# Gates, q and k as seven half products a pair, ahead of an attention in two token halves

## The chip, the core and the metric

The kernel runs on one core of a Trainium2 chip. The metric is the device time of one execution in microseconds (us); it is 1275.96 us before the change (median of 3 runs, 1275.76 to 1276.05). The engines are TensorE (PE in the profile, with its weight loads as PEld), VectorE (DVE), ScalarE (ACT), GpSimd (POOL) and SyncE (SP). SP and POOL also issue the DMA transfers; sixteen DMA engines move the bytes of both.

## The reference

One layer on 1024 tokens of width 1024, all in float32. What matters of it:

```python
h = rmsnorm(x, g_pre_mix)
proj = einsum('bsd,de->bse', h, w_in)            # u | q | k | v, 512 columns each
y_pool = einsum('bsc,cd->bsd', multiscale_pool(u_pool, w_pool_mix, pool_scale), w_br_pool)
# stick-breaking attention, 8 heads of 64, s < t only:
#   A[t,s] = sigmoid(z_ts) * prod_{s<j<t} (1 - sigmoid(z_tj)),  z = q k / 8,  o = A v
y_sb = einsum('bsc,cd->bsd', o_sb, w_br_sb)
gates = sigmoid(einsum('bsd,de->bse', h, w_gate) + b_gate)        # 2048 columns
merged = gates[..., :1024] * y_pool + gates[..., 1024:] * y_sb
x = x + rmsnorm(einsum('bsd,de->bse', merged, w_out), g_post_mix)
a = square(relu(einsum('bsd,df->bsf', rmsnorm(x, g_pre_mlp), w_up)))   # 4096 columns
x = x + rmsnorm(einsum('bsf,fd->bsd', a, w_down), g_post_mlp)
```

## The kernel before

**Layout and precision.** Activations lie transposed, channels on the 128 partitions and tokens along the free dimension, in two halves of 512 tokens. Every float32 operand is split into a rounded high part and the rest (`hi`, `lo`, both of the matmul type float32r), and every product is three matmuls: high x high, high x low, low x high (`mm3`, lines 107 to 117). A dense product of one 128-column group for one token half is 8 steps of three (`dense_steps`). The splits are a cast on ScalarE and a subtraction on VectorE.

**Who orders the work.** The program is written with a framework that allots buffers, sets every wait, and orders each engine's instructions: a planner plays the program through on a modelled time, and an engine gets the earliest written instruction that is ready then. On the chip each engine then runs its list strictly in that order, and so do the DMA queues of SP and POOL. `issue_after(i)` puts an instruction behind `i` on its engine.

**Stages.** `phase_in` loads x, splits it, and forms the four u groups, then q and k of the first pair of heads, with the pool windows on VectorE beside them. `phase_attention` runs over the 8 heads; for each, all eight rows of 128 query tokens: `att_scores` (z by two matmuls, then `F` = sigmoid(-z) and `T` = sigmoid(z) on ScalarE, a mask on POOL, a running product of F by a scan on VectorE, line 574, and a multiply of T by the shifted F, line 578), then `att_steps`, which transposes T on PE, splits it (lines 599 and 600) and multiplies it with v. Between these, a list of filler jobs (`fill`, `fillers`, `pump`) puts the other dense products: v, the other q and k pairs (`job_qk`) and the 16 gate groups (`job_gate`, each for both token halves, stored to DRAM as `gscr`). `phase_post` forms the branch products, multiplies them with the gates loaded back, merges, and forms the output product; `phase_mlp` and `down` follow.

**Seven products instead of eight.** The up product (from its second part on) and the down product use a seven-product scheme for 2 x 2 blocks. For the down product the sums of weight blocks are made ahead by DMA alone: `weight_sums` yields 32 transfers of 1 MiB from DRAM to DRAM on the POOL queue (line 1069 copies, line 1067 adds into the destination), into `wscr`. Before the change they are issued one at a time: after every second row of the attention scores, and the last four in `phase_post`.

```python
for add, out, src in (
    (False, s3, (0, 0)), (False, s1, (1, 0)), (True, s3, (1, 0)), (True, s1, (1, 1)),
    (False, s2, s3), (True, s2, (1, 1)), (False, s4, s2), (True, s4, (0, 1)),
):
    for q in range(4):
        ...
```

**PSUM.** Eight banks: two for dense products (`dps`), and in `zps` three for z, two for transposes, one for the attention's output.

Of the kernel before, what the change touches and what calls it, by code (L numbers as in the profile page):

```python
# [52 lines left out]
class Block:  # L53
    def __init__(self, tc, x, w, wmix, vec, eye, eyeb, maskb, rcnt, out):
# [3 lines left out]
        self.sched = []  # L58
# [4 lines left out]
        self.cut = 1024  # L63
        self.marks = []


    def prep(self, key, g, pieces=(), load=None, stash=None):
        nc = self.nc
        raw = self.wp.tile([P, 1024], F32, name="wraw", tag="wraw", bufs=2)
        if stash is None:  # L70
            hi = self.wp.tile([P, 1024], F32R, name="whi", tag="whi", bufs=3)
            lo = self.wp.tile([P, 1024], F32R, name="wlo", tag="wlo", bufs=3)
        else:
            t = self.hp.tile([P, 2, 1024], F32R, name="stash", tag=stash)
            hi, lo = t[:, 0, :], t[:, 1, :]
        edges = [0] + list(pieces) + [1024]
        for a, b in zip(edges, edges[1:]):
            c = slice(a, b)
            nc.sync.dma_start(raw[:, c], self.w[g][:, c])
            if load is not None:  # L80
                load()
            n = min(b - a, self.cut)
            for i in range(a, b, n):
                c = slice(i, i + n)
                nc.scalar.copy(hi[:, c], raw[:, c])  # L85
                self.last_lo = nc.vector.tensor_sub(lo[:, c], raw[:, c], hi[:, c].bitcast(F32)).ins  # L86
        self.prepped[key] = (hi, lo)
# [19 lines left out]
    def mm3(self, ps, terms, first=True, last=True):  # L107
        nc = self.nc
        n = len(terms)
        for i, (wh, wl, rh, rl) in enumerate(terms):  # L110
# [6 lines left out]
            nc.tensor.matmul(ps, wl, rh, start=False, stop=last and i == n - 1)  # L117
# [54 lines left out]
    def build(self):  # L172
        tc, nc = self.tc, self.nc
        self.table_inst = None
        order = [(("u", g), O_U + g) for g in (0, 1, 2, 3)]
        order += [(("q", 0), O_QK), (("k", 0), O_QK + 1)]
        self.fill = {
            -1: [("g", 0)],
            0: [("g", 8), ("g", 1)],
            1: [("q", 1), ("k", 1), ("g", 9)],  # L180
            2: [("g", 2), ("g", 10), ("g", 3, 0)],
            3: [("q", 2), ("k", 2), ("g", 3, 1), ("v", 0, 4)],
            4: [("v", 4, 32), ("g", 11)],
            5: [("g", 4), ("q", 3), ("k", 3)],
            6: [("g", 12), ("g", 5), ("g", 13, 0)],
            7: [("g", 13, 1), ("g", 6), ("g", 14), ("g", 7, 0)],
            8: [("g", 7, 1), ("g", 15)],
        }
        order += [(("v", 0, j), O_V + j) for j in range(2)]
        for h in range(-1, 9):  # L190
            for f in self.fill[h]:
                if f[0] == "v":
                    if f[1] == 0:
                        order += [(("v", 1, j), O_V + 2 + j) for j in range(2)]
                elif f[0] == "g":
                    if f[-1] != 1 or len(f) == 2:
                        order.append((f[:2], O_G + f[1]))
                else:
                    order.append((f, O_QK + 2 * f[1] + (f[0] == "k")))
        order += [(("br", e), O_BR + e) for e in range(8)]  # L200
        kept = {3: "t2_hi", 4: "t2_lo"}
        order += [(("out", 0, e), O_OUT + e, (), None, kept.get(e)) for e in range(8)]
        order += [(("out", 1, e), O_OUT + e) for e in (2, 1, 0)]
# [13 lines left out]
        self.wsums = self.weight_sums()  # L217
# [31 lines left out]


    def phase_in(self):
        tc, nc = self.tc, self.nc
        pa = tc.alloc_tile_pool(name="in_a", bufs=1, side="right")
        xs = [pa.tile([P, NK, H], F32, name=f"x{h}") for h in range(2)]
        mean = pa.tile([P, P], F32, name="mean")
# [1136 lines left out]
```

## Time and profile before

| | |
|---|---|
| time, median of 3 runs | 1275.96 us |
| span of the profiled execution | 1274.1 us |
| granted TensorE clock, mean | 1.000 |
| DMA packets moved | 233.70 MB, 183 GB/s on the mean |
| of it on the POOL queue (q0) | 88.49 MB, 23.7% of sixteen engines' span |
| of it on the SP queue (q1) | 144.04 MB, 33.9% |
| VectorE busy, 100 to 460 us (attention) | 278.75 of 360 us |
| ScalarE busy, 100 to 460 us | 199.00 of 360 us |

The page gives the busy time of each engine, the chain of work that ended last, and groups of instructions by line. A matmul's busy time overlaps that of its neighbours, since they are pipelined; the distance from one start to the next is what it costs. [...]

### The profile page before, as it was taken

The page shows a single profiled execution, that of the slowest core. Times are in us where ns is not written, and L with a number is a line of the kernel's source. Part 1 is how long each engine was busy: PE and PEld are TensorE (multiplying, and loading weights), DVE is VectorE, ACT ScalarE, POOL GpSimd, SP SyncE. Part 2 cuts the span into 40 slices and gives each one's busy share as a digit, 9 for nine tenths or more (in the row PEclk, how much of TensorE's full clock was granted, in tenths as well). Part 3 has the DMA queues.
Part 4 walks back from the last instruction along what each step waited for, and adds up shares of the span by engine and source line. Part 5 has one row for each costly group of instructions (what it writes and reads, how often), then busy time and mean ns, then how long its engine had stood idle before and what let it go on. Part 6 is the DMA issues. An engine that isn't in the chain of part 4 may idle for free.

```text
span 1274.1 us, 16614 instructions
## 1 busy us (share of the span) xinstructions
PE 1266.1 (99%) x6043; PEld 1057.7 (83%) x6043; DVE 924.9 (73%) x1315; ACT 614.6 (48%) x1022; POOL 169.6 (13%) x314
## 2 busy tenths in 40 slices
PE   9999999999999999999999999999999999999998
PEld 6898888889888888888878888888888888888887
DVE  8787688786878747551777988877775655776975
ACT  8235455564555542232456646455454433344452
POOL 1002213221223121100101002212120000001000
PEclk9999999999999999999999999999999999999999
DMA  6254447694686138671529578656559546556551
GB/s 226 67 165 166 146 161 163 138 219 141 124 215 223 67 120 232 198 219 33 182 85 303 183 247 277 219 198 208 199 205 346 193 154 223 189 179 238 199 220 67
DMA packets 75729, 233.70 MB, mean 183 GB/s; under 512 B 8608, under 2 KB 11168, under 8 KB 73472
## 3 DMA queue, kind: packets, MB, share of 16 engines
q1 hardware_dynamic: 48352, 144.04, 33.9%
q0 software_dynamic: 27152, 88.49, 23.7%
q8 instruction: 47, 0.77, 0.2%
q14 instruction: 34, 0.28, 0.1%
q10 hardware_dynamic: 144, 0.13, 0.0%
HBM read 178.10 MB, written 83.89 MB: 206 GB/s over the span
## 4 chain that ended last, share of the span: by engine, by line
PE 94%; DVE 3%; issue 1%; ACT 1%; DMA 1%; POOL 0%; SPq 0%; DVEq 0%; ACTq 0%; POOLq 0%
PE d L116 20%; PE d L117 20%; PE d L115 20%; PE dg L117 4%; PE dg L116 4%; PE dg L113 4%; PE o L616 3%; PE at L591 2%; PE dqk L116 2%; PE dqk L117 2%; PE dqk L113 1%; PE z L564 1%; PE z L561 1%; DVE F L574 1%; PE dv L117 1%
## 5 line engine op out<-in xcount | busy, mean ns | idle before, releaser
L116 PE MATMUL d<-blo,whi 128*128 128x512 f32 (+1 forms) x456 | 172.3, 378 | 0.0
L117 PE MATMUL d<-bhi,wlo 128*128 128x512 f32 (+1 forms) x456 | 171.9, 378 | 0.0
L115 PE MATMUL d<-bhi,whi 128*128 128x512 f32 (+1 forms) x456 | 168.7, 378 | 0.0
L574 DVE TENSOR_TENSOR_SCAN F<-F,past 128x256 f32<-128x256 f32 (+2 forms) x96 | 94.2, 981 | 20.9 <-ACT F L565 20.0
L85 ACT CAST whi<-wraw 128x512 fp32r<-128x512 f32 (+1 forms) x88 | 67.7, 799 | 77.2 <-PE d L116 38.0
L113 PE MATMUL dg<-hT_hi,whi 128*128 128x512 f32 x253 | 101.7, 402 | 0.0
L117 PE MATMUL dg<-hT_hi,wlo 128*128 128x512 f32 x256 | 100.8, 394 | 0.0
L116 PE MATMUL dg<-hT_lo,whi 128*128 128x512 f32 x256 | 100.4, 392 | 0.0
L117 PEld LDWEIGHTS d<-bhi,wlo 128*128 128x128 f32 x456 | 85.8, 188 | 15.9
L116 PEld LDWEIGHTS d<-blo,whi 128*128 128x128 f32 x456 | 85.7, 188 | 15.9
L115 PEld LDWEIGHTS d<-bhi,whi 128*128 128x128 f32 x456 | 85.5, 188 | 16.1
L86 DVE TENSOR_TENSOR wlo<-wraw,whi 128x512 fp32r<-128x512 f32 (+1 forms) x88 | 77.7, 905 | 28.4 <-ACT whi L85 28.3
L116 PE MATMUL d<-b_lo,whi 128*128 128x512 f32 x196 | 76.2, 390 | 0.4 <-DVE b_lo L836 0.4
L115 PE MATMUL d<-b_hi,whi 128*128 128x512 f32 x196 | 75.6, 389 | 0.0
L565 ACT ACTIVATE F<-z 128x256 f32<-128x256 f32 (+2 forms) x96 | 47.2, 493 | 58.8 <-DVE T L578 34.4
L117 PE MATMUL d<-b_hi,wlo 128*128 128x512 f32 x196 | 74.7, 389 | 0.0
L1124 DVE TENSOR_TENSOR wlo<-slots_hi,whi 128x1024 fp32r<-128x1024 f32 x29 | 35.5, 1225 | 53.1 <-ACT whi L1122 53.1
L600 DVE TENSOR_TENSOR alo<-at,ahi 128x512 fp32r<-128x512 f32 (+1 forms) x96 | 52.0, 553 | 29.9 <-ACT ahi L599 28.8
L1122 ACT CAST whi<-slots_hi 128x1024 fp32r<-128x1024 f32 x29 | 30.5, 1052 | 84.5 <-PE d L116 71.5
L599 ACT CAST ahi<-at 128x512 fp32r<-128x512 f32 (+1 forms) x96 | 45.1, 482 | 47.4 <-PE at L591 44.0
L1122 ACT CAST whi<-slots_lo 128x1024 fp32r<-128x1024 f32 x27 | 28.4, 1053 | 73.4 <-PE d L116 59.7
L578 DVE TENSOR_TENSOR T<-T,F 128x255 f32<-128x255 f32 (+3 forms) x96 | 53.1, 556 | 11.0 <-POOL T L568 2.5
(323 smaller groups left out, 3309.3 us busy)
## 6 DMA issues: line engine op xcount, KB each, us to landing
wraw<-w SPq DMA_DIRECT2D x80, 512.0 KB, 4.3
wscr<-w POOLq DMA_DIRECT2D x24, 1024.0 KB, 10.0
ext_b<-ascr SPq DMA_DIRECT2D x40, 512.0 KB, 4.3
gscr<-gs POOLq DMA_DIRECT2D x32, 256.0 KB, 4.2
gate<-gscr POOLq DMA_DIRECT2D x16, 512.0 KB, 4.5
pscr<-p SPq DMA_DIRECT2D x32, 256.0 KB, 3.2
braw<-w SPq DMA_DIRECT2D x16, 512.0 KB, 5.1
ascr<-c POOLq DMA_DIRECT2D x32, 256.0 KB, 5.0
```

Source lines behind the costliest of these rows:

```text
L85: nc.scalar.copy(hi[:, c], raw[:, c])
L86: self.last_lo = nc.vector.tensor_sub(lo[:, c], raw[:, c], hi[:, c].bitcast(F32)).ins
L113: nc.tensor.matmul(ps, wh, rh, start=first and i == 0, stop=False)
L115: nc.tensor.matmul(ps, wh, rh, start=first and i == 0, stop=False)
L116: nc.tensor.matmul(ps, wh, rl, start=False, stop=False)
L117: nc.tensor.matmul(ps, wl, rh, start=False, stop=last and i == n - 1)
L565: nc.scalar.activation(f[:, c : c + n], z[:, :n], AF.Sigmoid, scale=-1.0)
L574: nc.vector.tensor_tensor_scan(fr, fr, past[:, c : c + n][:, ::-1], 1.0 if top else f[:, c + n : c + n + 1], ALU.mult, ALU.max)
L578: nc.vector.tensor_mul(tl[:, c:e], tl[:, c:e], f[:, c + 1 : e + 1])
L599: nc.scalar.copy(hi[:, c:], at[:, c:])
L600: nc.vector.tensor_sub(lo[:, c:], at[:, c:], hi[:, c:].bitcast(F32))
L1122: last_split[0] = nc.scalar.copy(hi, src).ins
```

## The change

The parts of the work between the u products and the output product are rearranged.

- After u, v is formed for both token halves with 512 columns at once, scaled, and stored to DRAM (`vscr`). u too goes to DRAM (`uscr`).
- A new stage `phase_project` forms gates, q and k before the attention, as 12 pairs of output groups by seven half products. The activations' sums are made on VectorE in `phase_in`; the weights' sums are made by DMA (`sw_sums`, 24 transfers of 1 MiB, DRAM to DRAM) and loaded a pair ahead (`sw_weights`). Results go to DRAM (`qscr`, `gscr`).
- Beside these products a generator `later` loads v twice, one token apart, stores the split difference (`sscr`), computes the pool mixer from `uscr` (to `yscr`), and splits the branch and output weights and stores both parts (`hscr`). What passes through on-chip memory in it uses four staging buffers in turn (`staged`).
- The 32 transfers of `weight_sums` are issued in this stage, four behind the first result of each of the first eight pairs.
- The attention runs over all heads for the first 512 tokens, then over all heads for the others, with q and k loaded per head (`load_head`). It keeps only the running products of sigmoid(-z) and multiplies them with the differences of v; the second sigmoid, the mask and the multiply are gone. Fillers are now the pool branch products (`job_pool`), and in the second half the merge (`job_merge`) and output products (`job_out`) of the first token half. Branch and output weights come from `hscr`, already split.
- `phase_post` keeps the second token half. In the MLP the buffers of one stage are placed elsewhere.

```diff
+    PAIRS = [("q", 0), ("k", 0), ("q", 1), ("k", 1)] + [("g", i) for i in range(8)]
+    def sw_sums(self):
+        for n in range(3):
             ...
+            for out, x, y in ((s3, a21, a22), (s1, a11, a21), (s2, s3, a11), (s4, s2, a12)):
+                yield nc.gpsimd.dma_start(out, x)
+                yield nc.gpsimd.dma_start(out, y, accum_op=ALU.add)
+    def staged(self, shape, dt, name):
+        self.turn += 1
+        return self.mx.tile(shape, dt, name=name, tag=f"m{self.turn % 4}")
+    def result(self, kind, f, h, t, sign):
         ...
+        if kind == "g":
+            nc.scalar.activation(t, t, AF.Sigmoid, bias=self.vt[:, V_BG + f : V_BG + f + 1], scale=sign)
+            return nc.gpsimd.dma_start(self.gscr[f][:, c], t)
         ...
+        e = self.staged([P, 2, H], F32R, f"{kind}s")
         ...
+        return nc.gpsimd.dma_start(self.qscr[kind == "k"][f][:, :, c], e.bitcast(F32))
+    def later(self):
+        for t in range(NK):
+            pair = self.staged([P, 2, H], F32, "vpair")
+            for j in range(2):
+                nc.sync.dma_start(pair[:, j, :], self.vscr[t * P + j : t * P + j + P, :])
+            yield
             ...
+            nc.gpsimd.dma_start(self.sscr[t], v.rearrange("p h x -> p (h x)").bitcast(F32))
+            yield
         ...
+        for g in range(16):
+            raw = self.staged([P, 1024], F32, "hraw")
+            nc.sync.dma_start(raw, self.w[O_BR + g])
+            yield
+            hi, lo = (self.staged([P, 1024], F32R, "hw") for _ in range(2))
+            nc.scalar.copy(hi, raw)
+            nc.vector.tensor_sub(lo, raw, hi.bitcast(F32))
+            for t, scr in zip((hi, lo), self.hscr[g]):
+                nc.gpsimd.dma_start(scr, t.bitcast(F32))
+            yield
+    def phase_project(self):
         ...
+        def product(w, at, name):
+            pool, tag, n = next(banks)
+            d = pool.tile([P, H], F32, name="sw", tag=tag, bufs=n)
+            self.half(d, w, at, name)
+            next(nxt, None)
+            if i > 0:
+                next(bg, None)
+            return d
+        for i, (kind, f1) in enumerate(self.PAIRS):
             ...
+            nc.scalar.copy(u, product(w["a1"], 0, "b11"))
+            nc.vector.tensor_add(c11, u, product(w["a1"], 512, "b21"))
+            done = self.result(kind, f1, 0, c11, 1.0)
+            for _ in range(4):
+                with tc.issue_after(done.ins):
+                    next(self.wsums, None)
+            nc.vector.tensor_add(u, u, product(w["sb"], 0, "t2"))
+            nc.vector.tensor_add(v, u, product(w["sa"], 0, "t3"))
+            d = product(w["sa"], 512, "t1")
+            nc.vector.tensor_add(c22, v, d)
+            nc.vector.tensor_add(u, u, d)
+            self.result(kind, f2, 1, c22, -1.0)
+            nc.vector.tensor_add(v, v, product(w["a22"], 0, "t4"))
+            self.result(kind, f2, 0, v, -1.0)
+            nc.vector.tensor_add(u, u, product(w["sb"], 512, "b22"))
+            self.result(kind, f1, 1, u, 1.0)
+        self.run(bg)
         ...
+        for i in range(4):
+            for t, scr in zip(self.y, self.yscr[i]):
+                nc.gpsimd.dma_start(t[:, i, :].bitcast(F32), scr.bitcast(F32))
     def att_scores(self, h, i):
         ...
-            nc.scalar.activation(f[:, c : c + n], z[:, :n], AF.Sigmoid, scale=-1.0)
-            nc.scalar.activation(tl[:, c : c + n], z[:, :n], AF.Sigmoid)
         ...
+            f = tl[:, c : c + n]
+            self.after = nc.scalar.activation(f, z[:, :n], AF.Sigmoid, scale=-1.0)
         ...
-            nc.vector.tensor_mul(tl[:, c:e], tl[:, c:e], f[:, c + 1 : e + 1])
     def phase_attention(self):
         ...
+        jobs = [[self.job_pool(e, h), 4] for e in range(8) for h in range(2)]
+        tail = [[self.job_out(e), 8] for e in (6, 7)]
+        halves = [jobs[:14], jobs[14:] + [[self.job_merge(e, 0), 4] for e in range(8)] + [[self.job_out(e), 8] for e in range(6)]]
+        for g in range(2):
+            rows = (3, 2, 1, 0) if g == 0 else (7, 6, 5, 4)
             ...
+            if g == 0:
+                lead = 6
+                for _ in range(lead):
+                    self.advance()
```

More of the change, by code (lines that the diff above doesn't have):

```diff
@@ new lines, in phase_in, with normed @@
+        for h in range(2):
+            d = self.dps.tile([P, H], F32, name="du", tag="d")
+            self.dense(d, self.weights(("u", 3), 0), hT[h])
+            if h == 0:
+                v_weights(0)
+            u_out(3, [(h, d)])
+        for h in range(2):
+            columns(h)
+        for _ in range(16):
+            with tc.issue_after(self.last_u.ins):
+                next(sums)
+        x00, x01, x10, x11 = (xs[h][i : i + 4] for h in range(2) for i in (0, 4))
+        def normed(h, k):
+            nc.vector.scalar_tensor_tensor(
+                out=xs[h][k], in0=xs[h][k], scalar=self.gn[:, k : k + 1], in1=self.rb[h],
+                op0=ALU.mult, op1=ALU.mult,
+            )
@@ new lines, in mix_out, with job_out @@
+    def mix_out(self, mix, e, d, acc, first, pool, tag):
+        nc = self.nc
+        nc.scalar.copy(mix[e], d)
+        sq = acc if first else pool.tile([P, H], F32, name="sq", tag=tag, bufs=2)
+        nc.scalar.activation(sq, d, AF.Square)
+        if not first:
+            nc.vector.tensor_add(acc, acc, sq)
+    def job_out(self, e):
+        if e == 0:
+            self.mix0 = []
+            for i in range(4):
+                t = self.mx.tile([P, 2, H], F32, name=f"mix0_{i}", tag=f"m{i}")
+                self.mix0 += [t[:, 0, :], t[:, 1, :]]
+            self.rb = [self.rp.tile([P, H], F32, name=f"rb{h}", tag=f"rb{h}") for h in range(2)]
+        wt = self.weights(("out", 0, e))
+        d = self.bank()
+        yield from self.dense_steps(d, wt, self.mg[0])
+        self.mix_out(self.mix0, e, d, self.rb[0], e == 0, self.sp, "sq")
@@ L687, in phase_attention @@
-            out = self.att_steps(h, 0, [a[r] for r in range(4)])
+            self.queue = halves[g]
+            n = sum(f[1] for f in self.queue)
+            cost = {i: 0.25 * max(2, i + 1) / 2 for i in rows}
+            step = 0.9
+            total = 8 * (sum(cost.values()) + step * (4 * g + 4))
+            rate = n / total
+            self.w_out = step * rate
+            if g == 0:
+                lead = 6
+                for _ in range(lead):
+                    self.advance()
+            for h in range(8):
+                a = {}
+                for i in rows:
+                    a[i] = self.att_scores(h, i)
+                    self.pump(rate * cost[i])
+                    if out is not None:
+                        for _ in range(2 if g and h else 1):
+                            next(out, None)
+                if out is not None:
+                    self.run(out)
+                nh = 8 * g + h + 2
+                if nh < 16:
+                    self.load_head(nh % 8, nh // 8)
+                out = self.att_steps(h, g, [a[i] for i in rows[::-1]])
@@ L688, in phase_attention @@
         while self.queue:
             self.advance()
-        self.queue = self.fillers(8)
-        self.w_out = 3.0
-        for _ in out:
-            pass
+        self.queue = tail
+        self.w_out = 1.0
+        self.run(out)
         self.pump(self.w_out)
@@ L916, in chain, with half @@
             self.fill_operand("t4", k, b21)
-    def half(self, ps, wt, at, name):
+    def half(self, ps, wt, at, name, start=True, stop=True):
         wh, wl = wt
```

701 lines of the change are left out of this document (357 added, 344 removed).

## The prediction

> **What bounds the kernel now.** I read the page from the top: the span, the busy shares, then the chain that ended last.
>
> ```profile
> span 1274.1 us, 16614 instructions
> ...
> PE 1266.1 (99%) x6043; PEld 1057.7 (83%) x6043; DVE 924.9 (73%) x1315; ACT 614.6 (48%) x1022; POOL 169.6 (13%) x314
> ...
> PE 94%; DVE 3%; issue 1%; ACT 1%; DMA 1%; POOL 0%; SPq 0%; DVEq 0%; ACTq 0%; POOLq 0%
> ```
>
> PE is busy 99% of the span and 94% of the chain; nothing else holds the end. A matmul's busy time (389 ns) overlaps its neighbours', so the price of one is the step from start to start, in the timeline of PE:
>
> ```profile
> 90.04 0.28 PE L115 MATMUL dv<-whi,hT_hi 128*128 128x256 f32 x1
> ...
> 92.44 0.28 PE L117 MATMUL dv<-whi,hT_lo 128*128 128x256 f32 x1
> ...
> 850.06 0.39 PE L115 MATMUL d<-t_hi,whi 128*128 128x512 f32 x1
> ...
> 859.81 0.39 PE L116 MATMUL d<-t_lo,shi 128*128 128x512 f32 x1
> ```
>
> The last two rows are 43 matmuls apart: 9.75 / 43 = 0.2267 us for 512 columns. The first two are 20 apart: 0.120 us for 256 columns. A kernel whose only limit is PE gains what its matmuls lose, so the first half of the sum is a count. The second half asks whether PE stays the only limit, and for that I read the DMA side, which is cheap today because it is spread out.
>
> **Part 1: matmuls.** Gates and q, k are 24 output groups of 128 columns, today 24 x 2 x 8 x 3 = 1152 matmuls. As 12 pairs of 7 half products of 4 x 3 they are 1008. Removed: 144 x 0.2267 = 32.6 us. v changes from 384 matmuls of 256 columns (46.1 us) to 192 of 512 (43.5): 2.6 us. Scores, transposes, attention products, pool mix, branch, output and MLP keep their counts.
>
> ```profile
> L113 PE MATMUL dg<-hT_hi,whi 128*128 128x512 f32 x253 | 101.7, 402 | 0.0
> L117 PE MATMUL dg<-hT_hi,wlo 128*128 128x512 f32 x256 | 100.8, 394 | 0.0
> L116 PE MATMUL dg<-hT_lo,whi 128*128 128x512 f32 x256 | 100.4, 392 | 0.0
> ```
>
> Interleaved with the attention a triple takes 13 + 5 + 3 = 21 ns more than three at 389. 384 triples leave that mixture (-8.1 us) and 160 of branch, merge and output enter it (+3.4): -4.7 us. PE alone would give 1274.1 - 32.6 - 2.6 - 4.7 = 1234.2 us.
>
> **Part 2: the attention on VectorE.** The running products drop the second sigmoid, the mask on POOL and the multiply by F:
>
> ```profile
> L578 DVE TENSOR_TENSOR T<-T,F 128x255 f32<-128x255 f32 (+3 forms) x96 | 53.1, 556 | 11.0 <-POOL T L568 2.5 <-ACT T L566 1.4
> L574 DVE TENSOR_TENSOR_SCAN F<-F,past 128x512 f32<-128x512 f32 x40 | 50.4, 1259 | 7.6 <-ACT F L565 7.1
> L574 DVE TENSOR_TENSOR_SCAN F<-F,past 128x384 f32<-128x384 f32 x24 | 23.7, 988 | 5.4 <-ACT F L565 5.2
> L574 DVE TENSOR_TENSOR_SCAN F<-F,past 128x256 f32<-128x256 f32 x24 | 16.7, 697 | 5.7 <-ACT F L565 5.5
> L600 DVE TENSOR_TENSOR alo<-at,ahi 128x512 fp32r<-128x512 f32 (+1 forms) x96 | 52.0, 553 | 29.9 <-ACT ahi L599 28.8
> L600 DVE TENSOR_TENSOR alo<-at,ahi 128x512 fp32r<-128x512 f32 x48 | 32.6, 687 | 19.5 <-ACT ahi L599 18.7
> L627 DVE TENSOR_TENSOR oT<-o,ou 64x256 f32<-64x256 f32 x32 | 13.4, 417 | 3.6 <-ACT ou L625 2.8
> 66.86 0.60 PE L345 MATMUL rt<-eye,rb 128*128 128x128 f32 x4
> 67.22 0.48 PE L115 MATMUL dm<-ph,wmh 128*128 128x512 f32 x1
> 750.00:800.00 50.00, 50.00 (x223) 41.38 (x222) 46.64 (x72) 30.63 (x46) 10.81 (x20) 1.00 0.76 253
> ```
>
> That is worth nothing by itself, since PE hides it. But the attention also gets shorter, because gates, q, k and v leave it. In the second token half DVE has scans 32 x 1.259 + 16 x 0.988 + 16 x 0.697 = 67.3, the low parts 40 x 0.687 + 24 x 0.404 = 37.2 (0.404 is the mean of the 48 narrower ones), outputs 16 x 0.417 = 6.7, and 36 operations of 0.687 for merge, splits and sums = 24.7: 136 us. PE has there scores 23.8, 208 transposes at 0.09 (the step 66.86 to 67.22 over four) 18.7, products 24.8 and 264 filler matmuls 59.8: 127 us. DVE becomes the bound by 9 us at full use, by 19 at the 93% of the busiest 50 us of MLP work shown above. I take +13. The first half (DVE 61, PE 66) stays with PE. In the projection DVE has about 181 us beside 234 of PE, ScalarE less; both are covered, and if PE waits they are covered the more.
>
> **Part 3: the DMA engines in the projection.** All 32 weight-sum transfers of the down product (wscr), today spread over 109 to 546 us, go four to a pair into the first eight pairs; 24 new 1 MiB sums for gates, q and k come on the same POOL queue; and u, v, q, k, the shifted v, the pool output and the split branch and output weights all pass through DRAM. The prices, in busy time of all sixteen DMA engines, come from stretches that hold one kind of transfer alone (columns: stretch, PE, PEld, DVE, ACT, POOL, clock, DMA share, GB/s):
>
> ```profile
> 239.00:249.00 10.00, 10.00 (x54) 8.39 (x53) 8.59 (x14) 6.42 (x14) 2.22 (x3) 1.00 0.67 107
> 290.00:300.00 10.00, 10.00 (x83) 9.88 (x82) 8.07 (x14) 4.60 (x12) 2.10 (x5) 1.00 0.29 105
> 218.00:230.00 12.00, 12.00 (x64) 10.07 (x63) 9.28 (x15) 7.24 (x16) 4.32 (x7) 1.00 1.06 198
> 970.00:980.00 10.00, 10.00 (x46) 8.28 (x45) 4.72 (x4) 4.01 (x4) 0.00 (x0) 1.00 1.02 415
> 210.00:230.00 20.00, 20.00 (x106) 16.86 (x105) 16.26 (x27) 12.01 (x27) 7.31 (x12) 1.00 0.94 180
> ```
>
> One accumulating MiB: 0.67 of 10 us = 6.7 us. One copied MiB, DRAM to DRAM: 2.9 us. Plain loads and stores saturate at 415 GB/s: 2.53 us a MiB. Between the first u stores and the first pool product of the attention the changed kernel must move: 28 accumulations (12 new, 16 moved) 188 us; 28 copies (12 and 16) 81 us; POOL stores and loads, in MiB u 2, v 2, q and k 8, gates 8, shifted v 4, pool 4 and 4 back, split weights 16 = 48; SP loads, pair weights 21, v weights 2.5, v pairs 4, u 2, raw weights 8, heads 1.5 = 39; the 87 MiB take 220 us. Sum 488 us. Full use shows as 1.02 to 1.06, so at 1.04 it needs 469 us.
>
> None of that can go beside something later. The attention's first products read y, whose loads stand last on the POOL queue behind all of it, and that queue is served in order:
>
> ```profile
> 218.15 1.18 POOL L1067 DMA_DIRECT2D wscr<-w  x1
> 218.81 1.10 POOL L521 DMA_DIRECT2D gscr<-gs  x1
> ...
> DMA to landing us min/median/max: 2.3/4.4/11.3
> ...
> 40.48 1.28 DVE L389 TENSOR_TENSOR u<-du,rb 128x512 f32<-128x512 f32 x2
> ```
>
> The gate store behind the accumulation is the 11.3 us one; free, it takes 2.3. The u products leave PSUM at 40.5 us, so the stores start at 41 and the attention at 41 + 469 = 510. PE, unhindered, would be there at 5.4 (its first matmul) + (384 + 1032) x 0.2267 + some 2 = 328: u and v, the 1008, the pool mix. **PE waits 182 us.** The waits come where result and staging buffers (four slots) are held by stores queued behind four accumulations, 27 us against a pair's 84 x 0.2267 = 19 us of PE: pairs 2, 3, 5, 7.
>
> The Trainium skill, in "DMA: Bandwidth & Descriptors", section "Anatomy of one DMA", fits a transfer as 2.0 us plus its bytes at 436 GB/s, which makes any MiB 4.4 us and an accumulation no dearer than a copy. The trace disagrees: 1 MiB copies of wscr land in about 5.5 us but accumulations in about 10, and 6.7 against 2.9 us busy. By that rule the sum would be smaller; it is rival C.
>
> Sum: 1234.2 + 13 + 182 = 1429 us of span; the median of the runs shown is 1275.96, 1.9 over the profiled span: **1431 us**. Ends: DMA at 1.06 and DVE +9 gives 1418; at 0.94 (the 20 us stretch above) 488 / 0.94 = 519, attention at 560, DVE +19: 1487.
>
> **Rivals.**
> A, faster: the planner, which issues what is ready, lets the wscr transfers (no reader until the down product) and the eight output weight granules fall behind the y loads. Then 488 - 16 x 6.7 - 16 x 2.9 - 30 = 304, at 1.04 292 us: the attention starts at 333 instead of 328, and the time is 1254 us. For it: wscr has no early reader. Against: the code puts each four right behind the pair's first store, and today they are issued just where the code has them. It decides at 298 us of DMA work ahead of the attention.
> B: only wscr falls behind: 334 / 1.04 = 321, attention at 362, +34: 1283 us.
> C: an accumulation occupies the engines like a copy: 488 - 28 x 3.8 = 382 / 1.04 = 367, attention at 408, +80: 1329 us.
> D: waiting makes PE slow. The first nine matmuls of the run, after idleness, stand 0.45 us apart:
>
> ```profile
> 1.43 4.02 PE L313 MATMUL idle<-zero 128*128 128x512 bf16 x9 [1.43 <-DVE zero L310]
> ```
>
> If PE stays at that pace through the projection, 1032 x 0.447 = 461 us from 94 on ends at 555, 45 us after the DMA: 1476 us.
> The Trainium skill, "TensorE: Matmul & The Clock Gate", Part 1, says that the clock halves after an idle window of about 3.4 us; by it D happens in each long wait, but mostly under the DMA's cover.
> E: the buffers hide the gap and DVE costs nothing: 1236 us, the change doing what its count says; against it, 143 MiB would have to pass in the 287 us from 41 to 328: 522 GB/s, where the saturated stretch shows 415.
>
> **How the numbers follow.** Forecast, 1400 to 1475: 0.52. D and worse: 0.13. B, C and between, 1279 to 1400: 0.20. A and E, faster: 0.12. Within 0.2% (what a measurement of this kernel can tell from no change): 0.03. So faster 0.12, same 0.03, slower 0.85. The range leaves out A, E and the far end of D: 1280 to 1500.
>
> **What would show it.** Right: PE busy falls to 5 or 6 tenths in the slices from about 100 to 510 us, the DMA digits stand at 9 there, PE's waits name DVE and ACT, theirs name stores (qscr, sscr, yscr), and gate stores land after 20 us and more; matmul records fall by 336; in the second attention half DVE is at 9. Wrong: DMA share in the projection below 0.8 (A or E), accumulations landing under 6 us (C), or matmul steps of 0.45 us there (D). The count of Part 1 fails if dense steps differ from 0.2267 us.

## The result, and the profile after

The changed kernel takes 1606.3 us (median of 4 runs, 1602.0 to 1611.2) where the kernel before took 1275.9 in the same measurement: the ratio is 1.259, 95% interval 1.2565 to 1.2615. The forecast was 1431 with a range up to 1500. The direction was right, the size was not.

The page of the profile after, its parts 1 to 4 (busy time, the span in forty slices of 40.1 us each, the two large DMA queues, the chain):

```profile
span 1604.7 us, 16545 instructions
...
PE 1286.0 (80%) x5707; PEld 1043.0 (65%) x5707; DVE 945.3 (59%) x1299; ACT 615.6 (38%) x982; POOL 231.2 (14%) x413
...
PE   9955885818790200788899999999999999999998
...
DVE  8434553304461211568976478878777756576786
...
PEclk9976997868895555899999999999999999999999
DMA  5999999997967677676741686586655585465661
...
DMA packets 126916, 359.58 MB, mean 224 GB/s; under 512 B 15024, under 2 KB 20144, under 8 KB 124560
...
q1 hardware_dynamic: 78928, 202.77, 39.0%
q0 software_dynamic: 47760, 155.62, 31.9%
...
PE 21%; DMA 0%; DVE 0%; ACT 0%; issue 0%; SPq 0%; DVEq 0%
```

There are 336 matmuls fewer (6043 to 5707), as counted. But PE, 99% busy before, has a hole in the slices from 481 to 642 us (digits 0, 2, 0, 0) and is thin from 80 us on, with a 1 in the slice from 321 to 361 us; and 359 MB are moved instead of 234. The chain says little here: PE carries 21% of it and the other shares are 0%, so most of it is unattributed. The stretches have to be read one by one.

The table by stretch (columns as in the prediction: length, PE, PEld, DVE, ACT and POOL busy, granted clock, DMA share, GB/s; a DMA share of 1.00 is all sixteen DMA engines busy all the time). The cuts are the marks of the work: first product of gates, q and k at 98.9 us, the last at 484.1, the first and the last load of a weight granule at 530.4 and 633.3, the first scores at 649.4:

```profile
41.00:98.00 57.00, 57.00 (x257) 47.13 (x256) 22.82 (x33) 12.17 (x17) 19.41 (x25) 1.00 0.99 275
98.00:484.00 386.00, 261.42 (x1028) 207.04 (x1027) 164.87 (x228) 106.19 (x148) 83.57 (x120) 0.82 0.95 267
484.00:530.00 46.00, 4.21 (x10) 2.02 (x9) 10.03 (x15) 3.03 (x4) 2.69 (x5) 0.56 0.63 218
530.00:640.00 110.00, 8.59 (x22) 5.77 (x21) 20.50 (x18) 17.40 (x17) 19.66 (x37) 0.53 0.77 258
...
650.00:968.00 318.00, 292.63 (x1428) 235.73 (x1427) 231.84 (x352) 148.83 (x332) 42.23 (x106) 0.98 0.59 193
...
41.00:649.00 608.00, 331.23 (x1313) 261.96 (x1311) 218.67 (x294) 138.79 (x186) 125.88 (x188) 0.76 0.89 262
```

Up to 484 us the DMA engines are nearly full and PE is two thirds busy: the shape that was forecast. From 484 to 649 nothing is full. PE has almost nothing to do, no engine is busy for a quarter of it, and the DMA share is 0.63 to 0.79. That looks like a chain, in which one thing waits for the next; e2 below tests it. The waits name its links (the last three rows are waits inside the products; columns: who waits, line, for whom; us in total, times, the longest):

```profile
PE z L722 <- DMA qq<-qscr: 89.9, 1, 89.9
ACT hw L615 <- DMA hraw<-w: 79.8, 14, 7.2
SPq L612 <- DMA hscr<-hw: 76.3, 14, 7.7
PE dm L104 <- ACT ph L596: 39.8, 1, 39.8
PE sw L104 <- ACT u L651: 37.1, 1, 37.1
PE sw L104 <- ACT whi L1086: 33.9, 4, 16.2
PE sw L104 <- ACT ev L416: 31.5, 2, 29.4
```

PE waits 40 us for the last pool group and, after a few branch products, 90 us for the first head's q, which stands on SP's queue behind sixteen weight granules, since it uses their staging buffers. Each granule's load waits for the stores of one before it to land (14 waits, 76 us), and each cast waits for its load (14 waits, 80 us). A view of the granules' line shows the pace:

```profile
L612 SPq DMA_DIRECT2D hraw<-w x16: 327/328/338, 530.4 to 633.3; - x16
```

Sixteen loads in 102.9 us are one every 102.9 / 15 = 6.9 us, for 1.5 MiB moved each. The four buffers hold one granule (three buffers) and the load of the next, so by this reading the round trip sets the pace, not the engines.

Where the 176 us beyond the forecast's span of 1429 came from:

| stretch | forecast | after | more |
|---|---|---|---|
| to the first scores | 510 | 649.4 | 139 |
| attention and post, to the first up product | 293 | 313 | 19 |
| up, down and the end | 626 | 643 | 17 |

(293 is what the forecast of 1429 leaves: 1429 - 510 - 626, where 626 is the trace of before from its first up product, 648.4, to its end.)

### The profile page after: what moved, and what is told of

It reads as the page before. It is cut to its first block, busy times and chain, and to the rows that moved or that the text cites. A ratio compares the mean times of both kernels' runs of the same rounds, so it can differ in the third digit from the quotient of the medians.

```text
span 1604.7 us, 16545 instructions
## 1 busy us (share of the span) xinstructions
PE 1286.0 (80%) x5707; PEld 1043.0 (65%) x5707; DVE 945.3 (59%) x1299; ACT 615.6 (38%) x982; POOL 231.2 (14%) x413
## 5 line engine op out<-in xcount | busy, mean ns | idle before, releaser
L722 PE MATMUL z<-kk,qq 128*128 128x256 f32 (+2 forms) x96 | 33.5, 358 | 90.9 <-DMA qq<-qscr 89.9
L104 PE MATMUL sw<-h_hi,whi 128*128 128x512 f32 x144 | 60.0, 418 | 54.1 <-ACT ev L416 31.5
L728 DVE TENSOR_TENSOR_SCAN T<-T,past 128x256 f32<-128x256 f32 (+3 forms) x96 | 90.0, 966 | 10.8 <-ACT T L727 9.6
L722 PEld LDWEIGHTS z<-kk,qq 128*128 128x128 f32 x96 | 18.3, 192 | 94.6 <-issue 90.3
L616 DVE TENSOR_TENSOR hw<-hraw,hw 128x1024 fp32r<-128x1024 f32 x16 | 19.6, 1225 | 88.4 <-ACT hw L615 58.4
L104 PEld LDWEIGHTS sw<-h_hi,whi 128*128 128x128 f32 x144 | 28.9, 201 | 62.4 <-ACT ev L416 32.6
L727 ACT ACTIVATE T<-z 128x256 f32<-128x256 f32 (+3 forms) x96 | 43.8, 496 | 42.6 <-PE z L725 25.1
L105 PE MATMUL sw<-h_lo,whi 128*128 128x512 f32 x144 | 59.3, 412 | 0.0
L106 PE MATMUL sw<-h_hi,wlo 128*128 128x512 f32 x144 | 58.0, 406 | 0.2
```

The source lines that it names most:

```text
L104: nc.tensor.matmul(ps, wh, rh, start=first and i == 0, stop=False)
L105: nc.tensor.matmul(ps, wh, rl, start=False, stop=False)
L106: self.last_mm = nc.tensor.matmul(ps, wl, rh, start=False, stop=last and i == n - 1).ins
L616: nc.vector.tensor_sub(lo, raw, hi.bitcast(F32))
L722: m = nc.tensor.matmul(zz, qq[:, 0, tt], k[:, cols], start=True, stop=False)
L727: self.after = nc.scalar.activation(f, z[:, :n], AF.Sigmoid, scale=-1.0)
```

## The experiments

To be told apart were three causes of the 139 us ahead of the first scores: DMA work beside the products, a chain behind them that has its own length whatever the products take, and waits by the order of a queue. Each expectation names its theory and rival. The times below are device times beside 1275.4 to 1278.7 us for the kernel before; stretches come from the trace of one execution each, by the same marks as above, and are good to 1 us.

| run | time, us | ratio, 95% interval | products | gap to first scores | first scores to last output product | from there to first down product |
|---|---|---|---|---|---|---|
| changed kernel | 1606.3 | 1.2565 to 1.2615 | 385 | 165 | 319 | 317 |
| e1 | 1537.4 | 1.2005 to 1.2090 | 287 | 144 | 359 | 326 |
| e2 | 1513.6 | 1.1793 to 1.1930 | 385 | 62 | 320 | 331 |
| e3 | 1424.2 | 1.1123 to 1.1200 | 284 | 40 | 358 | 321 |
| e4 | 1539.0 | 1.2026 to 1.2096 | 326 | 163 | 317 | 313 |
| e5 | 1597.0 | 1.2455 to 1.2568 | 394 | 148 | 316 | 316 |
| e7 | 1595.2 | 1.2436 to 1.2559 | 381 | 162 | 315 | 313 |
| e8 | 1416.8 | 1.1063 to 1.1136 | 312 | 41 | 327 | 316 |
| e9 | 1380.4 | 1.0783 to 1.0846 | 241 | 42 | 355 | 322 |
| e10 | 1383.9 | 1.0784 to 1.0893 | 260 | 48 | 335 | 323 |
| e11 | 1388.1 | 1.0791 to 1.0952 | 241 | 44 | 360 | 321 |
| e12 | 1380.9 | 1.0780 to 1.0850 | 259 | 52 | 334 | 320 |
| e13 | 1396.8 | 1.0911 to 1.0975 | 242 | 44 | 366 | 325 |
| e14 | 1377.0 | 1.0755 to 1.0832 | 242 | 25 | 359 | 329 |
| e15 | 1396.1 | 1.0912 to 1.0976 | 242 | 40 | 359 | 336 |

The down part, from its first matmul to the last of the run, is 314.8 us in every one, as before the change.

**e1: the down product's sums later.** The 32 `wscr` transfers leave the projection; one goes to each head of the attention in each token half, and the other 16 are written into the first part of up. They are tied only to the last gate load, though, and the planner had them issued earlier: in e1 from 803 to 884 us, twelve of them ahead of up's first product at 870 and all ahead of the last output product at 888.

```diff
             done = self.result(kind, f1, 0, c11, 1.0)
-            for _ in range(4):
-                with tc.issue_after(done.ins):
-                    next(self.wsums, None)
...
                     self.pump(rate * cost[i])
+                    if i % 4 == 2:
+                        with tc.issue_after(self.last_in.ins):
+                            next(self.wsums, None)
```

> The 32 transfers into wscr leave the projection: 16 go one by one into the attention, 16 into the up product. Theory (the DMA engines are full until about 500 us, then a serial chain through four staging buffers holds the attention's start at 649 us): 16 x 6.7 + 16 x 2.9 = 154 us of DMA work leave, the products end near 340 instead of 484 us, the chain of v, pool and the sixteen weight granules, no longer slowed by the queue, ends at 390 to 440, and the time is 1390 to 1440 us, some 20 of it from a fuller attention. Rival (the tail from 484 to 649 us belongs to the planner's order and follows the products whatever they take): products 100 to 140 us earlier, tail still 165 us, time 1470 to 1500 us.

Measured 1537.4. The products shrink from 385 to 287 us, but the tail stays (144), and the stretch from the first scores to the last output product is 40 us longer, up 9. The rival was right about the tail, which is shorter by only 21 us for all the DMA work taken from the products; for the sums in their new place the theory had some 20 us, the rival named none.

Where the 40 us lie can be read from the trace. From the first scores to the last product with v it takes 244 us, 242 in the changed kernel, with 13 transfers of the sums in it. From there to the last output product it takes 115 us instead of 77, with the 16 others in it. So the sums beside the attention cost some 2 us, and those behind it some 38.

**e2: no split granules.** The branch and output weights are loaded raw and split where they are used, as before the change; the sixteen granules of `later` are gone.

```diff
-            for t, scr in zip((hi, lo), self.hscr[g - O_BR]):
-                nc.sync.dma_start(t[:, cols].bitcast(F32), scr[:, cols])
+            raw = self.wp.tile([P, 1024], F32, name="wraw", tag="wraw", bufs=2)
+            nc.sync.dma_start(raw[:, cols], self.w[g][:, cols])
+            nc.scalar.copy(hi[:, cols], raw[:, cols])
+            self.last_lo = nc.vector.tensor_sub(lo[:, cols], raw[:, cols], hi[:, cols].bitcast(F32)).ins
```

> Branch and output weights are loaded raw and split where they are used, as in the kernel before; the sixteen granules of the generator and their stores are gone. Theory (the tail is a chain of sixteen granules of 6.9 us through four staging buffers, latency and not bandwidth): 16 x 6.9 = 110 us of the tail go, the time is 1470 to 1510 us, with some 36 us of splits more on VectorE in the attention. Rival (the tail too is bandwidth, DMA share 0.70 there): only the 61 us of DMA work of the granules go, time 1540 to 1560 us.

Measured 1513.6, 4 us over the theory's range. The gap falls by 103 us, the 102.9 that the granules took in the trace of the changed kernel, and the products stay at 385. The DMA work of the granules, 61 us by the expectation and 77 as measured below, would not make 103. So the granules cost their own chain and little else. Table by stretch of e2 (columns as above), products and gap:

```profile
98.00:483.00 385.00, 261.72 (x1026) 207.93 (x1025) 166.36 (x231) 107.53 (x151) 83.56 (x120) 0.83 0.94 266
...
483.00:545.00 62.00, 11.91 (x31) 6.74 (x30) 10.77 (x16) 3.83 (x5) 4.83 (x9) 0.57 0.69 224
```

**e3: both.**

> Both edits. Theory: 488 - 154 - 61 = 273 us of DMA work are left ahead of the attention, 287 at the share of 0.95 seen, so it could start at 328 us, which is PE's own pace; with the start of the projection still waiting 30 us for stores behind the sums, it starts at 350 to 390 us and the time is 1290 to 1340 us. Rival (half clock and the attention's own waits are the larger part): no lower than 1400 us.

Measured 1424.2. Products (284) and gap (40) gain what e1 and e2 gained, and the stretch behind keeps e1's extra 40 us: PE's waits from the first scores to the last output product are 60 us against 25 in the changed kernel. By its total the rival was right; a part of what the move gained in the products was lost again behind the attention (105 us there, 73 in e2).

**e4: accumulations as plain copies.** The additions of all weight sums are left out, so the sums are not formed; the number and size of transfers are the same.

```diff
-                yield nc.gpsimd.dma_start(out, y, accum_op=ALU.add)
+                yield nc.gpsimd.dma_start(out, y)
...
-                    self.nc.gpsimd.dma_start(out[q], a, accum_op=ALU.add)
+                    self.nc.gpsimd.dma_start(out[q], a)
```

> All 28 accumulating transfers (12 for gates, q and k, 16 for the down product) are plain copies of the same size: the additions of the weight sums are left out. Theory (an accumulation holds the DMA engines 6.7 us, a copy 2.9): 28 x 3.8 = 106 us of DMA work go, 112 at the share of 0.95, the products end near 380 us and the time is 1480 to 1510 us. Rival (what counts is the number of transfers and their order in the queue, not how long each occupies the engines): time 1580 to 1606 us.

Measured 1539.0, 67 us less and between theory and rival; 59 of it are in the products (385 to 326). An accumulation is dearer than a copy, but by less than priced: DMA work up to the first scores is 0.84 x 545 = 458 us here and 0.89 x 608 = 541 in the changed kernel, 83 us for 28 accumulations, or 3.0 us each where the prediction had 6.7 - 2.9 = 3.8.

```profile
41.00:586.00 545.00, 323.18 (x1307) 257.22 (x1305) 217.27 (x293) 138.33 (x186) 112.56 (x188) 0.79 0.84 292
```

**e5: the granules first.** The granules are taken ahead of the v pairs and the pool mixer in `later`; no work is added or left out.

```diff
     def later(self):
+        for g in range(16):
+            raw = self.staged([P, 1024], F32, "hraw")
+            ...
         for t in range(NK):
             pair = self.staged([P, 2, H], F32, "vpair")
```

> All work as in the changed kernel; the sixteen weight granules are taken first in the side work of the projection instead of last, so that they can pass beside the first pairs' products. Theory (the tail after the products is a serial chain through four staging buffers at a DMA share of 0.70, while the DMA engines set the pace before it): the transfers ahead of the attention, 0.95 x 459 + 0.70 x 152 = 542 us of all sixteen engines, pass at 1.04 in 521 us, attention from 562 instead of 649, 1510 to 1535 us. Rival (granules and products cost the same wherever they stand, because q and k results use the same four buffers and the pairs then wait for them): the products end later by what the tail loses, 1580 to 1620 us.

Measured 1597.0, in the rival's range. The products take 394 us at a DMA share of 1.01 and the gap is still 148, now with the pool mixer and the loads of y in it:

```profile
98.00:493.00 395.00, 252.38 (x1014) 201.85 (x1012) 159.89 (x207) 113.53 (x151) 93.22 (x138) 0.82 1.01 299
493.00:641.00 148.00, 26.28 (x45) 12.28 (x45) 36.32 (x54) 13.48 (x18) 12.30 (x23) 0.51 0.50 170
```

The waits of PE in the same run name it:

```profile
PE dm L104 <- ACT ph L606: 65.9, 4, 52.5
PE dbr L104 <- DMA yhi<-yscr: 33.8, 4, 10.7
```

Whichever part of the side work comes last, the attention waits for it; reordering only changes its name.

**e7: v's stores on SP.** The 29 us wait at the start of the projection (`ev`) is for stores that stand behind weight sums on POOL's queue.

```diff
-            nc.gpsimd.dma_start(self.vscr[1 + t * P : 1 + t * P + P, :], s)
+            nc.sync.dma_start(self.vscr[1 + t * P : 1 + t * P + P, :], s)
```

> All work as in the changed kernel; only the eight stores of v are issued on SP's queue instead of POOL's, past the weight sums that stand there. Theory (the DMA engines set the pace of the projection, so a wait removed at its start comes back later): the 29 us that PE waits for v's eviction buffers at the start go, the products end at most 10 us earlier, 1593 to 1606 us. Rival (the wait is a pure loss by the queue's order): products end 30 us earlier, 1570 to 1580 us.

Measured 1595.2, in the theory's range. The longest `ev` wait falls from 29.4 to 11.6 us, but the products end only 4 us earlier: while the DMA engines are full, a wait that is removed comes back as another (here `whi`, 33.9 to 44.5).

**e8 and e9: the sums of gates, q and k on VectorE.** `sw_sums` and its 24 DMA transfers are gone; the two raw granules of a pair are split, and then summed in place by four additions of 512 columns. e8 is e2 with this, e9 is e3 with this.

```diff
+        w["a22"] = self.split_weights(r2[:, 512:], pool, f"a{i % 2}", 1, 512)
+        a11, a12, a21, a22 = r1[:, :512], r1[:, 512:], r2[:, :512], r2[:, 512:]
+        nc.vector.tensor_add(a22, a21, a22)
+        nc.vector.tensor_add(a21, a11, a21)
+        nc.vector.tensor_add(a11, a22, a11)
+        nc.vector.tensor_add(a12, a11, a12)
+        w["sb"] = self.split_weights(r1, pool, f"s{i % 2}", 1)
```

> No split granules in DRAM, as in e2_no_granules, and the 24 transfers that sum the weights of gates, q and k in DRAM are replaced by four VectorE additions of 512 columns a pair, on the raw weights in place (48 x 0.69 = 33 us of VectorE). DMA work falls by 12 x 6.7 + 12 x 2.9 + 9 MiB x 2.53 = 138 us. Theory (DMA sets the pace): the products, 384 us in e2, lose 88 (at the 0.64 us per us that e1 returned) to 138, and the rest stays: 1376 to 1426 us. Rival (the preparation of weights on ScalarE and VectorE through two raw buffers becomes the wait): less than 50 us, 1465 us or more.

> As e3_both (no granules, the down product's sums later), with the sums of gates, q and k on VectorE as in e8. The DMA engines are then at less than half of their time in the projection, so that only PE and the preparation of weights are left there. Theory: products of 284 us in e3 fall to 240 to 250, the rest stays, 1380 to 1392 us. Rival (of e3's 43 us of waits in the projection the most are for the preparation of weights, not for transfers): 1410 to 1425 us.

Measured 1416.8 and 1380.4: both in the theory's range. In e9 the products take 241 us; 1034 matmuls at 0.2267 us are 234 of it. Tables by stretch, e8 first:

```profile
98.00:410.00 312.00, 249.92 (x1029) 200.43 (x1028) 186.34 (x269) 102.28 (x141) 75.93 (x112) 0.91 0.86 258
```

and e9:

```profile
98.00:339.00 241.00, 236.82 (x1034) 194.31 (x1033) 187.66 (x272) 105.04 (x145) 48.37 (x84) 0.99 0.57 197
```

PE is at 98% with the clock at 0.99, once the DMA share is 0.57. The loss of the projection was the DMA work beside it. The sums that the seven products need are a large piece of it: e8 against e2 is 97 us (73 in the products, 21 in the gap) for 33 us of VectorE that PE hides. Where the down product's sums have already left, in e9 against e3, they are 44. DMA work to the first scores falls from 0.92 x 504 = 464 (e2) to 0.78 x 410 = 320 us (e8): 144, where the prices of the prediction give 138.

**e10: the down product's sums spread** over e9: 8 beside u and v, 12 one to a pair, 12 one to a head; v's stores on SP.

> As e9 (no granules in DRAM, sums of gates, q and k on VectorE), with the 32 transfers of the down product's weight sums spread: 8 beside the u and v products, 12 one to a pair, 12 one to a head of the attention; v's stores on SP. Theory (what the transfers cost is what they collide with: the projection of e9 has a DMA share of 0.55 and takes 12 more, and the attention of e9, 355 us with 16 copies and sums in it against 327 in e8 without, has fewer): projection 241 to 252, attention 330 to 345, 1355 to 1372 us. Rival (each accumulation holds the POOL queue wherever it stands, and the stores and loads behind it wait): 1378 us or more.

Measured 1383.9, the rival's range. The stretch from the first scores on is 20 us shorter, the products 19 longer, the gap 6 longer. The 20 us are not what the theory had in mind. The e9 that it speaks of has 30 of the 32 transfers in that stretch and not 16, since here too the planner issued those written into up ahead of it, from 662 to 735 us with up's first product at 737:

```profile
662.41 1.97 POOL L1195 DMA_DIRECT2D wscr<-wscr  x4
```

PE waits 29 us from the last product with v to the last output product, 8 in e8. The most of it is for weights:

```profile
PE d L106 <- ACT whi L71: 19.4, 2, 17.0
```

This stretch takes 106 us in e9 with 16 transfers in it, and 80 in e10 and in e8 with none. From the first scores to the last product with v it takes 249 us in e9 with 14, 247 in e8 with none. So beside the attention 13 or 14 of these sums cost 2 to 6 us (e1, e3 and e9, each against the run without; e10 has 255 us with 10), while beside the products and behind the attention they are dear. No run left all of them beside the attention, where the kernel before has 28.

**e11 and e12: no branch products ahead of the scores** (`lead = 6` becomes 0), on e9 and on e10.

> As e9, with none of the pool mix's branch products ahead of the first scores (six steps before). Theory (in the gap of 42 us between the products and the first scores PE stands 21 us before a branch product that waits for y, the last load on the POOL queue, with the scores behind it in PE's order): the gap falls to some 20 us, 1355 to 1366 us. Rival (the scores' own inputs, or the products that are put off, wait as long a little later): 1374 to 1384 us.

> Both edits of e10 and e11. Theory: the gains add, 1332 to 1352 us; still over the kernel before, since some 20 us of gap, 60 us of an attention slower than its matmuls and the post part stay, and the products' 33 us of saved matmuls do not cover them. Rival: 1365 us or more.

Measured 1388.1 and 1380.9; the theory fell in both. The gap stays, 44 and 52 us, with another name: the 21 us wait for y is now part of a wait for q.

```profile
PE z L695 <- DMA qq<-qscr: 43.2, 1, 43.2
```

That is e11. Its timeline of SP's queue shows why: v's eight transfers, 4 MiB, are issued before the first heads' loads are through.

```profile
335.10 2.43 SPq L673 DMA_DIRECT2D kk<-qscr  x4
337.63 1.08 SPq L671 DMA_DIRECT2D qq<-qscr  x1
338.75 8.70 SPq L653 DMA_DIRECT2D v<-sscr  x8
349.60 0.45 SPq L672 DMA_DIRECT2D qq<-qscr  x1
```

**e13: an order that did not take.** e11 with v's loads tied behind the last head load written, and y's behind v's.

```diff
+        for t in range(NK):
+            with tc.issue_after(last):
+                v = nc.sync.dma_start(
```

> As e11, with the loads at the end of the projection put in another order: the first two heads' q and k, then v (SP's queue), then the pool output y (POOL's queue). Theory (the gap of 42 to 44 us is an order of loads: in e11 the eight v transfers of 512 KB and the gate's stand ahead of the small head loads, which land 4 to 20 us after their issue): the scores start some 20 us earlier, 1358 to 1370 us. Rival (the gap is the price of what must be loaded before the attention can run, v, y and the heads, some 9 MiB x 2.53 = 23 us and the waits for the buffers that the products held until then; the first attention products wait for v and the branch products for y instead): the gap is shorter and the attention longer by as much, 1376 us or more.

Measured 1396.8, but the trace shows v's loads still ahead of most of q's: the planner had put the load named by `last` among the first five. The run says nothing about the order that was meant; a tie to one instruction fixed only that one.

**e14 and e15: heads before v, for good.** e14 chains every early head load to the one before it and v behind them, and takes the down product's sums from the first two heads (two more are written into up). e15 has the second edit alone. Of the three sums that stand in the gap of e11 (335 to 337 us) the traces of both still have one, at 338 and 339 us: the planner had issued the third head's there.

```diff
+            with self.tc.issue_after(self.last_head) if pool and self.last_head else contextlib.nullcontext():
+                self.last_head = nc.sync.dma_start(out.bitcast(F32), src).ins
```

> As e11, with each load of the first heads' q and k issued in a fixed order ahead of v's eight loads on SP's queue, and with no weight sum of the down product before the third head (two more of them fall into the up part). Theory (the gap is an order: small head loads behind 4 MiB of v and behind 1 MiB sums): the first scores start 15 to 25 us earlier than in e11 (gap 20 to 28 us instead of 44), 1358 to 1372 us. Rival (the gap is bandwidth and buffers: the last pool output must be stored before q and k may take its staging buffers, and v and y must come in after the last product): gap 38 us or more, 1376 to 1390 us.

> As e14, with the loads left in the order of e11: only the weight sums before the third head are taken away. Theory of order: the gap falls by half of what e14 gains or less, 36 to 42 us. Rival by collision (the three 1 MiB transfers that stand in the gap of e11, 10 to 20 us from issue to landing, hold the last pool output's stores on POOL's queue behind them): the gap falls as far as in e14, to 20 to 28 us, and the time to 1358 to 1372 us.

The gap is 25 us in e14 and 40 in e15, both in the range of the theory of order; the total of e14, 1377.0, is over its range, and e15 measured 1396.1. So of the last 40 us some 15 are the order of the loads, and two of the three sums in the way are worth some 4 at most; the third was not taken away. The rest is most likely what must come in: e14's gap has a full DMA share, one sum included.

```profile
340.00:365.00 25.00, 1.53 (x7) 0.94 (x5) 0.69 (x1) 0.72 (x1) 3.19 (x6) 0.63 1.03 313
```

The profiled executions are some 10 and 16 us longer than the gaps alone would give against e11 (spans of 1373.2 and 1394.6 against 1382.5 less 19, and less 4): up is 8 and 15 us longer. In both, two of the sums are issued behind up's first product and in e11 none, but that they are the cause was not shown. e14, e9 and e12 are the fastest versions found; all are still some 8% slower than the kernel before, so none beats it.

## Why the prediction was right or wrong

**Part 1, the count: right.** 336 records went, and with the DMA work out of the way (e9) the 1008 half products take 241 us with the pool mix, 4.2 of them waits.

**Part 2, VectorE in the attention: the right size, in part by luck.** PE's waits for VectorE there are small and many; from 650 to 900 us of the changed kernel:

```profile
PE at L744 <- DVE alo L753: 7.2, 9, 1.6
PE o L768 <- DVE alo L753: 5.3, 5, 2.9
PE o L768 <- DVE oT L784: 3.7, 5, 1.8
```

These three make 16 us where +13 was taken. But 6 of them come before 745 us, in the first token half, which the prediction gave to PE, and in the second half VectorE is busy for 96 of 115 us (745 to 860), so it delays PE there without being the bound throughout. The stretch came out 19 us over the forecast, which also had nothing for matmul steps at less than the full clock (some 13 us in it, an estimate by their distances from start to start).

**Part 3, the DMA engines: the right bound, and the step that failed.** "Full use shows as 1.02 to 1.06, so at 1.04 it needs 469 us" and "the attention at 41 + 469 = 510" treat all transfers up to the attention as one load on a full server. Two things in it were wrong, the amount and the use, and they add up to the 139 us.

- The amount. It was 0.89 x 608 = 541 us, not 488: at 1.04 that is 520 us and a start at 561, 51 us later. The sums were not the cause. e4 has an accumulation 3.0 us dearer than a copy, not 3.8. e1, in whose trace 13 copies and 16 accumulations have left this stretch, lowers the work from 541 to 0.84 x 488 = 410, by 131 where the prices say 145. The plain transfers were more, and dearer. The transfers from 41 to 649 us other than sums are 96 MiB (262 GB/s x 608 us are 152, of them 56 sums), where the prediction has 87: among others it left out the loading of v's differences (4 MiB) and took 1.5 MiB for the heads, which are 3.5. And e2, which moves 25.5 MiB less (against 263 GB/s x 504 us), has 77 us less work, 3.0 us a MiB where 2.53 was taken:

```profile
41.00:545.00 504.00, 330.63 (x1310) 261.80 (x1309) 199.09 (x279) 123.66 (x173) 107.79 (x154) 0.81 0.92 263
```

  By these prices 96 MiB are 288 us where the prediction has 220, and the accumulations 22 us less: 46 of the 53 us. Why a plain MiB is dearer here than in the saturated stretch of before was not tried.
- The use. 88 us (649 less 561) are lost because the engines were not full. Up to 484 us they were nearly so, at 0.99 and 0.95: (0.05 x 57 + 0.09 x 386) / 1.04 = 36 us. Behind it 541 - 0.99 x 57 - 0.95 x 386 = 118 us of work, 113 at full use, took 165: 52 us. For the granules each load waits for a store before it, and the time is links times round trip, 15 x 6.9 us. e2 shows it: without them 103 us of the gap go and the products do not change.

The sentence "None of that can go beside something later" was right, and more binding than the sum made of it: the order that puts y and q last makes the attention wait for the end of the chain, not for the bytes.

"The waits come where result and staging buffers ... are held by stores queued behind four accumulations" was right for a part of the products' waits: `u` (37.1 us) and `ev` (31.5) are such waits. Some 49 us more are waits for the preparation of weights (`whi` and its like), which the sentence does not name. That a wait removed there brings little (e7) fits the full engines.

**Rivals.** A and B did not happen: the planner left the sums with the pairs. C did not hold: an accumulation is dearer than a copy, by 3.0 us instead of the 3.8 priced. Nor does e4, where all are copies, come near its time (1539 against 1329), because the tail and the plain transfers stay. E did not happen. D was there in small: from 98 to 484 us the granted clock is 0.82, and the steps of 0.33 to 0.7 us there exceed the full-clock step by some 26 us in all; how much of that the DMA engines would have hidden anyway was not separated. The Trainium skill, "TensorE: Matmul & The Clock Gate", Part 1, has the clock come back after about 3.4 us of work; the trace agrees roughly. Behind waits of 16.4 us (at 546.73) and 4.5 us the steps are 0.43 us, and 4.65 us after the second they are 0.23:

```profile
553.30 0.80 PE L106 MATMUL dbr<-yhi,wlo 128*128 128x512 f32 x1 [4.52 <-DMA wlo<-hscr]
...
556.45 0.63 PE L104 MATMUL dbr<-yhi,whi 128*128 128x512 f32 x1
556.88 0.63 PE L105 MATMUL dbr<-ylo,whi 128*128 128x512 f32 x1
...
557.95 0.39 PE L104 MATMUL dbr<-yhi,whi 128*128 128x512 f32 x1
558.18 0.40 PE L105 MATMUL dbr<-ylo,whi 128*128 128x512 f32 x1
```

**The MLP: a term that was missing.** Up is 323.3 us from its first product to the first of down, 306.4 before (17 more). 22 matmuls of the output product stand between its first ones (5 us), and PE waits 8.8 us in it where it waited 0.4 before; the rest, some 3 us, is slower steps. The waits are for the split of the weights, the largest:

```profile
PE d L106 <- DVE slo L1087: 4.4, 3, 1.9
```

By the table's marks up varies from 313 (e4, e7) to 336 (e15). The sums issued in it are not enough to explain that: e14 and e15 have two, but e2, with none in it, has 331. Why the splits come late stays open; whether the newly placed buffers do it was not tried.

**The signs.** Of what was to show the steps, PE's digits are 5 to 9 with one 1 (two thirds busy), the DMA digits stand at 9 up to 361 us and then at 7, 9 and 6, PE's waits name ScalarE and VectorE, and theirs name stores. VectorE is at 8 and 9 tenths for two slices, 722 to 802 us, and lower before and after, so it binds only in part of the attention's second half. One sign failed: gate stores do not land after 20 us and more; from 100 to 480 us it is the stores of q that take longest (issues, size of one, median us to landing):

```profile
qscr<-qs POOLq DMA_DIRECT2D x8, 512.0 KB, 19.6
...
gscr<-c POOLq DMA_DIRECT2D x16, 256.0 KB, 5.7
...
gscr<-v POOLq DMA_DIRECT2D x7, 256.0 KB, 13.7
```

**What the forecast's range missed.** Its upper end, 1500, came from bounds on prices and use that all shared one picture, a full server. It had no case for a chain behind the products (52 us) nor for more and dearer plain transfers (most of the 51).

## What to carry to other kernels

The busy time of the DMA engines gives the earliest end of a stage, not its end: add the last dependent chain (by the reading of this case, its links times the landing time of a load, the work and the landing time of the store, divided by the granules that its buffers hold at once), and ask what stands behind it on the same queue or in the same buffers. When PE is 99% busy, a saving of matmuls that is paid in transfers through DRAM has to be priced against the stage where those transfers fall; here 33 us of matmuls were bought with 126 MB. Sums of weights that must be loaded anyway were better made on an engine with room (33 us of hidden VectorE in place of 24 transfers, which gained 97 us in e8 and 44 in e9). And the place where the code writes a transfer need not be where it is issued: read it from the trace before a stretch is blamed on it, as the 16 sums that were meant for up show.

## What the runs showed of the hardware

Landing times follow what is on the way at the same time, not the kind of transfer alone. Part 6 of the changed kernel's page (size of one, median us from issue to landing):

```profile
wscr<-w POOLq DMA_DIRECT2D x24, 1024.0 KB, 20.9
...
swscr<-w POOLq DMA_DIRECT2D x18, 1024.0 KB, 15.7
```

The same rows of e4, where none of these transfers adds (in the kernel before, where they are issued one at a time, the sixteen copies into `wscr` land in 5.2 to 9.2 us):

```profile
wscr<-w POOLq DMA_DIRECT2D x24, 1024.0 KB, 17.4
...
swscr<-w POOLq DMA_DIRECT2D x18, 1024.0 KB, 9.9
```

The Trainium skill, "DMA: Bandwidth & Descriptors", section "Anatomy of one DMA", has 2.0 us plus the bytes at 436 GB/s, an estimate of 4.4 us for such a transfer by that page; the rows are two to five times that, and nothing in the fit stands for what else is on the way.

In e11 a head load of 128 KB lands 3.2 us after its issue when little stands ahead, and up to 19.8 us after it behind v's 4 MiB (the loads of q from 335 to 395 us):

```profile
DMA to landing us min/median/max: 3.2/4.2/19.8
```
